# A two-layer trunk on one core: modulation split over three engines, norm rows between the first chains, last gate inside the first output tile, steps and loads moved

## The chip, the cores and the metric

The kernel runs on 1 core of one Trainium2 chip. TensorE (PE) multiplies, VectorE (DVE), ScalarE (ACT) and GpSimd (POOL) work on tiles in SBUF and PSUM, SyncE (SP) issues most DMAs. The metric is the device time of the core in microseconds (us), as the median of several executions.

## The reference

Two layers over 2080 tokens (a prompt of 2048 and a sample of 32) of width D = 1024. Every layer is `x + gate * rmsnorm(mixer(rmsnorm(x) * (1 + scale) + shift))`; shift, scale and gate come from the conditioning vector through one matrix `ada_w` of 1024 x 3072 a layer. Layer 0 mixes with a real-gated linear recurrence, layer 1 with forgetting attention.

```python
shift, scale, gate = split(silu(c) @ ada_w[i] + ada_b[i], 3)
h = rmsnorm(x, norm_pre[i]) * (1 + scale) + shift
# layer 0: 12 blocks of 128 of 1536 channels
xb, g = split(h @ lru_w_in, 2)
xc = conv4(xb)
r, ig = sigmoid(xc @ w_a + b_a), sigmoid(xc @ w_x + b_x)   # block by block
a = exp(-8 * r * softplus(-lam))
hs = scan(a, sqrt(1 - a * a) * ig * xc)
y = (hs * silu(g)) @ lru_w_out
# layer 1: 16 heads of 64, the sample also sees a cache of 512 rows
q, k, v, g, fl = split(h @ fox_w_in)
cum = cumsum(log_sigmoid(fl + b_f))
y = (softmax(q k^T / 8 + cum_q - cum_k, causal) @ v * silu(g)) @ fox_w_out
x = x + gate * rmsnorm(y, norm_post[i])
```

## The kernel before

**Precision.** A matrix is split into a rounded part (hi) and the rest (lo). `hi_pool` (L98, POOL) or `hi_act` (L95, ACT) writes hi, `lo_dve` (L104, a subtraction with two SBUF inputs on DVE) writes lo. A product is three matmuls: hi x hi, lo x hi, hi x lo, of 128 columns by 512.

**Order.** The code is written as generators which one Python program steps by hand; `yield` is a place where other work may be issued. A scheduler then places instructions by their dependences and by when buffers come free. Buffers come from pools with few slots each (roles `ahalf` 11 slots, `w` 5, `raw` 3, `half` 5, `h` 32, `c` 12, `wg` 2); a tile waits until the slot's last reader is done. Every engine and SP's queue run in order.

**0 to 56 us: first modulation.** `ada(0, (0, 2, 1, 3))` reads 32 tiles of 128x512 of `ada_w` (L243), with 8 loads ahead. Every third tile is `whole`: PE takes it as plain fp32 (L296 with `scf`). The other 21 are split: hi on POOL, lo on DVE, two matmuls each (L296 with `scs`). After 8 tiles `finish` adds (L259, L260), PE transposes the result (L269) and DVE writes the scales `gsv` (L276) or shifts `shv`. `prenorm` loads the first 1024 rows of `x` in four groups of 256, takes sums of squares (`stats`, L346 to L350), scales the rows (L353), transposes them on PE (L372), modulates them on ACT (L378) and splits them into `h`.

**56 to 729 us: layer 0's input.** `lru_in` runs over 12 blocks for each half of the tokens: `chain` (L556, 24 matmuls for 512 tokens), `gates` (L569), activations and the scan. Beside it run `norm_ahead` (norms the second half's rows into DRAM), `mod` (the rest of the modulations), `cache_parts` (splits the K and V cache), and `load_wout` (reads and splits w2, the output matrix of layer 0).

**729 to 1095 us: output of layer 0.** `out_tiles` takes 17 tiles of 128 tokens: 72 matmuls (L725) over 12 blocks into two banks (`pj`, `st`), as 36 pairs; `z` of a tile is loaded and split one tile ahead. When a tile is done, `norm_tile` norms its rows for layer 1: DVE writes `xn` (tile `c`, L445), PE transposes it in eight steps (L452) between the next tile's matmuls. The last modulation, layer 1's gate (`last`, 16 plain fp32 matmuls L296 into `pvb`), is stepped beside this.

**1095 to 2885 us: layer 1.** `proj` (V in L962, Q, K and gates in L1001) runs for the first half, then merged with attention. Attention is 640 steps of a 128-key tile each: scores (L1181, L1185), exponent on ACT (L1187, L1188), lo on DVE (L104), hi x hi sum on POOL (L1210), values (L1233, L1234). A unit's queries come by `q_load` into `ahalf` slots; its maxima (L1147) need `ext_d`, a DRAM tile. `LOAD_STEPS` is how many steps of the main stream pass between a job's loads and its first maxima. From 2680 us on, `out_tiles` of layer 1 (L725, tiles 0 to 6) run beside the last attention steps, with weights from `load_wout(w3)`; ten more tiles follow alone.

## Time and profile before

| | |
|---|---|
| median of 3 executions | 3035.75 us (3032.63 to 3041.42) |
| profiled execution, its own time | 3031.66 us |
| span of the profiled execution | 3029.7 us |
| PE busy in it | 2869.4 us, 95% |
| DVE, ACT, POOL busy | 1837.2, 1465.3, 1255.6 us |
| mean granted clock of PE | 0.985 |

The span is the time from the first to the last instruction of one execution. Where PE is busy 95% of it, time can be gained by closing what PE waits for, by fewer matmuls, or in stretches where its clock was granted below 1.00.

### The profile page before, as it was taken

What the parts mean: (1) busy time and instruction counts of PE and PEld (TensorE: products, weight loads), DVE (VectorE), ACT (ScalarE), POOL (GpSimd) and SP (SyncE); (2) the same over time, 40 slices, a digit from 0 to 9 for tenths busy, and PEclk for the clock granted to TensorE, in tenths of its full rate; (3) what the DMA queues carried; (4) which work ended last, traced back from release to release, by engine and by line L of the source; (5) the groups of instructions that cost most, each with busy time, mean ns of one, the idle gap of its engine ahead of it and who ended that gap; (6) DMA issues with size and microseconds to landing.
All of it is one profiled execution on the core that took longest, in us unless ns stands there. A gap on an engine that the chain in (4) does not pass through costs nothing.

```text
span 3029.7 us, 45098 instructions
## 1 busy us (share of the span) xinstructions
PE 2869.4 (95%) x14948; PEld 2293.8 (76%) x14948; DVE 1837.2 (61%) x3282; ACT 1465.3 (48%) x2962; POOL 1255.6 (41%) x1166
## 2 busy tenths in 40 slices
PE   6999999999999989999999999999999999989998
PEld 3777788897666677777777677887888788766776
DVE  7688777777432335646554565766776676676622
ACT  4565544556333333535354443665566556555621
POOL 5445443333222232434343332554555545455632
PEclk9999999999999999999999999999999999998999
DMA  7565675443644587676776776556555556464243
GB/s 277 197 220 199 218 270 192 151 152 127 191 135 129 161 302 254 187 247 187 222 220 210 227 222 192 147 176 154 152 155 152 165 148 176 131 164 121 82 135 96
DMA packets 407002, 548.40 MB, mean 181 GB/s; under 512 B 77096, under 2 KB 241064, under 8 KB 406768
## 3 DMA queue, kind: packets, MB, share of 16 engines
q1 hardware_dynamic: 406768, 545.50, 59.1%
q8 instruction: 119, 1.95, 0.3%
q14 instruction: 115, 0.94, 0.1%
HBM read 333.13 MB, written 212.22 MB: 180 GB/s over the span
## 4 chain that ended last, share of the span: by engine, by line
PE 38%; DMA 8%; DVE 6%; issue 5%; POOL 4%; ACT 3%; SPq 1%; POOLq 0%; DVEq 0%; ACTq 0%
PE pj L1001 13%; PE pj L962 4%; PE mx L1147 4%; PE st L1185 3%; PE st L1181 3%; PE pva L1233 3%; PE pvb L1234 3%; DVE ahalf L104 2%; DMA rc<-dn_d 1%; POOL ahalf L1210 1%; DVE mxs L1150 1%; PE pj L725 1%; DMA ahalf<-q_d 1%; POOL half L754 1%; PE mx L1376 1%
## 5 line engine op out<-in xcount | busy, mean ns | idle before, releaser
L1210 POOL TENSOR_TENSOR ahalf<-ahalf,ahalf 128x512 f32<-128x512 f32 (+2 forms) x528 | 582.5, 1103 | 418.7 <-ACT ahalf L1187 405.1
L1001 PE MATMUL pj<-h,w 128*128 128x512 f32 (+1 forms) x2304 | 585.3, 364 | 1.2 <-DVE half L104 1.2
L1187 ACT ACTIVATE ahalf<-st 128x512 fp32r<-128x512 f32 (+3 forms) x640 | 341.3, 533 | 376.0 <-PE st L1185 327.7
L104 DVE TENSOR_TENSOR ahalf<-st,ahalf 128x512 fp32r<-128x512 f32 (+3 forms) x640 | 386.9, 606 | 206.9 <-ACT st L1188 192.7
L1001 PEld LDWEIGHTS pj<-h,w 128*128 128x128 f32 x2304 | 424.5, 191 | 83.9 <-DVE half L104 1.4
L1150 DVE TENSOR_REDUCE mxs<-mx 128x1 f32<-128x512 f32 (+3 forms) x640 | 372.2, 605 | 148.0 <-PE mx L1147 84.9
L1188 ACT ACTIVATE st<-st 128x512 f32<-128x512 f32 (+3 forms) x640 | 339.8, 531 | 0.0
L1181 PE MATMUL st<-ahalf,kv 128*128 128x512 f32 (+3 forms) x640 | 244.0, 381 | 24.0 <-DVE ahalf L104 17.0
L1233 PE MATMUL pva<-ahalf,vs 128*128 128x512 f32 (+3 forms) x640 | 240.9, 388 | 10.8 <-POOL ahalf L1200 6.6
L962 PE MATMUL pj<-w,h 128*128 128x256 f32 (+3 forms) x1296 | 234.3, 288 | 12.1 <-DVE flog L977 5.4
L1185 PE MATMUL st<-ahalf,kb 96*128 96x512 f32 (+3 forms) x640 | 242.6, 386 | 1.0 <-ACT ahalf L1168 0.6
L1234 PE MATMUL pvb<-ahalf,vs 128*65 128x512 f32 (+3 forms) x640 | 228.1, 366 | 5.7 <-DVE od L1262 3.5
L1147 PE MATMUL mx<-kb,qm 96*128 96x512 f32 (+3 forms) x640 | 225.4, 384 | 7.2 <-DMA ext_d<-half 6.1
L556 PE MATMUL pj<-h,w 128*128 128x512 f32 (+1 forms) x1032 | 226.0, 369 | 0.8 <-POOL h L98 0.7
L962 PEld LDWEIGHTS pj<-w,h 128*128 128x128 f32 (+1 forms) x1296 | 192.3, 187 | 24.7 <-issue 7.5
L556 PEld LDWEIGHTS pj<-h,w 128*128 128x128 f32 x1032 | 177.3, 192 | 32.6 <-POOL h L98 0.9
L104 DVE TENSOR_TENSOR ahalf<-ahalf,ahalf 128x512 fp32r<-128x512 f32 (+2 forms) x183 | 143.9, 788 | 92.6 <-ACT ahalf L95 59.1
L104 DVE TENSOR_TENSOR w<-raw,w 128x1024 fp32r<-128x1024 f32 (+3 forms) x85 | 104.7, 1232 | 150.1 <-ACT w L95 68.5
L1001 PE MATMUL pj<-h,raw 128*128 128x272 f32 (+1 forms) x576 | 188.5, 327 | 0.0
L98 POOL TENSOR_SCALAR w<-raw 128x1024 fp32r<-128x1024 f32 (+3 forms) x68 | 76.1, 1120 | 251.5 <-DMA raw<-in_wqkg 54.2
L725 PE MATMUL pj<-h,ahalf 128*128 128x512 f32 (+1 forms) x408 | 168.2, 413 | 10.4 <-DVE ahalf L104 5.4
L1181 PEld LDWEIGHTS st<-ahalf,kv 128*128 128x128 f32 x640 | 121.7, 190 | 69.2 <-DVE ahalf L104 37.8
(325 smaller groups left out, 5615.5 us busy)
## 6 DMA issues: line engine op xcount, KB each, us to landing
wp_d<-w SPq DMA_DIRECT2D x60, 512.0 KB
vs<-v_d SPq DMA_DIRECT2D x96, 256.0 KB
kv<-k_d SPq DMA_DIRECT2D x192, 128.0 KB
ahalf<-q_d SPq DMA_DIRECT2D x192, 128.0 KB
raw<-in_w SPq DMA_DIRECT2D x44, 512.0 KB
ahalf<-in_ada_w SPq DMA_DIRECT2D x64, 256.0 KB
hb_d<-wg SPq DMA_DIRECT2D x32, 512.0 KB
v_d<-half SPq DMA_DIRECT2D x64, 256.0 KB
```

Of the source, the lines that this page charges most:

```text
L104: dve.tensor_tensor(o, i, f(h), ALU.subtract)
L556: pe.matmul(ps[:, :b - a], l, cols(r, a, b), start=i == 0, stop=i == 23)
L962: pe.matmul(ps[:m, :nw], l, r, start=c == 0, stop=c == 23)
L1001: pe.matmul(ps[:, :b - a], l, cols(r, a, b), start=c == 0, stop=c == 23)
L1147: pe.matmul(ps[:sw, :kw], u.qm[0:96, s0:s0 + sw], kb, start=True, stop=not last)
L1150: dve.tensor_reduce(u.mxs[:sw, si, c:c + 1], ps[:sw, :kw], axis=AX.X, op=ALU.max)
L1181: pe.matmul(ps[:kw, c0:nq], j.ka[k0 // 512][:, kc:kc + kw], u.qa[:, c0:nq], start=True, stop=False)
L1185: pe.matmul(ps[:kw, c0:nq], j.kb[k0 // HALF][0:96, kd:kd + kw], u.qb[0:96, c0:nq], start=False, stop=True)
L1187: act.activation(ph[:kw, c0:nq], ps[:kw, c0:nq], AF.Exp, scale=0.125)
L1188: act.activation(ps[:kw, c0:nq], ps[:kw, c0:nq], AF.Exp, scale=0.125)
L1210: pool.tensor_tensor(u.acc[:kw, c0:nq], f(ph)[:kw, c0:nq], u.acc[:kw, c0:nq], ALU.add)
L1233: pe.matmul(u.pva[:, c:nq], vs[:kw, 0:128], ph[:kw, c:nq], start=ti == 0, stop=last)
```

## The change

Nothing of the arithmetic's amount changes, but for the first modulation's `whole` tiles.
- First modulation: no tile is whole. All 32 get hi on ACT; lo is on POOL for tiles 0, 3, 6, ... (11 tiles, a two-input subtraction, new) and on DVE for the other 21.
- Rows of the first half: groups 2 and 3 are loaded before the first modulation ends into `c` slots, their stats follow group 1, and their transposes are issued between the matmuls of the first chains (`fill`).
- `norm_ahead` and `cache_parts` load one or two pieces ahead, the cache into `ahalf` slots (`cx`).
- `out_tiles`' first load and split stand ahead of the tail of layer 0's last block; the last gate's weights go into `w` slots, five ahead, and one of its matmuls is stepped per k (before, one per three).
- `norm_tile` has two more yields between `xn` and its transposes.
- The loads of `h` for V are spread: the first 512 tokens in the last output tile, the others between V steps.
- `LOAD_STEPS` 10 to 18, `q_load` two steps earlier, and w3 loaded two ahead with pauses, from the last projection unit on; two pauses ahead of the first output tile of layer 1.

```diff
...
-ADA_FIRST, ADA_LAST = 8, 6
+ADA_FIRST, ADA_LAST = 8, 5
...
-LOAD_STEPS = 10
+LOAD_STEPS = 18
...
                     a, b = get("ap", [128, 512], F32R), get("ap", [128, 512], F32R)
-                    hi_pool(a, t)
+                    (hi_act if ahead > 6 else hi_pool)(a, t)
+                    if ahead > 6 and i % 3 == 0:
+                        pool.tensor_tensor(b, t, f(a), ALU.subtract)
+                        parts[i] = (a, b)
+                        return
                     lo_dve(b, t, a)
...
                 for i in range(np_):
-                    x = get("xn", [w, pw])
+                    x = get("xn" if gi < 2 else "any", [w, pw])
                     sp.dma_start(x, src[t0 + 128 * t:t0 + 128 * t + w, pw * i:pw * i + pw])
...
-        ahead = 2
-        for gi in range(ahead):
+        for gi in range(2):
             load(gi)
-        done = 0
+        for gi in range(2):
+            stats(gi)
+        yield 0.0
+        for gi in range(2, len(groups)):
+            load(gi)
+        yield 0.0
         for gi, (t0, n, w) in enumerate(groups):
-            while done < min(gi + (1 if gi == 1 else 2), len(groups)):
-                stats(done)
-                done += 1
-            yield 0.0
+            if gi == 2:
+                stats(2)
+                stats(3)
+                yield 0.0
             xn = [xq.pop((gi, t)) for t in range(n)]
...
                 yield 110 * n
-            if gi + ahead < len(groups):
-                load(gi + ahead)
             flags.add(("n", layer, half, gi))
...
         groups = [(HALF + 256 * g, 2, 128) for g in range(4)] + [(SEQ, 1, NS)]
-        for t0, n, w in groups:
+        rows = []
+        def load(t0, n, w):
             xs = [[get("ahalf", [w, 512]) for _ in range(2)] for _ in range(n)]
...
                     sp.dma_start(xs[t][i], src[t0 + 128 * t:t0 + 128 * t + w, 512 * i:512 * i + 512])
-            yield
+            rows.append(xs)
+        load(*groups[0])
+        yield
+        for gi, (t0, n, w) in enumerate(groups):
+            xs = rows.pop(0)
             ss, rs = sm([128, 2, 2], "ss"), sm([128, 4], "rs")
...
                     dve.tensor_scalar(xs[t][i], xs[t][i], rs[:w, t:t + 1], None, ALU.mult)
+            if gi + 1 < len(groups):
+                load(*groups[gi + 1])
             g = 1 if t0 == SEQ else 0
...
         yield
+        yield
+        yield
         for k0 in (0, 4):
...
-    def lru_in(half, h, bank, gbank, lc, before):
+    def lru_in(half, h, bank, gbank, lc, before, fill=None):
...
                     i += 1
+                if fill is not None:
+                    next(fill, None)
...
         load(0)
+        yield 0.0
         if not half:
...
-    def load_wout(src, kn, w):
+    def load_wout(src, kn, w, ahead=0):
+        raw = {}
+        def load(k):
+            if k < kn:
+                raw[k] = get("raw", [128, D])
+                sp.dma_start(raw[k], src[128 * k:128 * k + 128, :])
+        for k in range(ahead):
+            load(k)
+        if ahead:
+            yield 0.0
         for k in range(kn):
-            t = get("raw", [128, D])
-            sp.dma_start(t, src[128 * k:128 * k + 128, :])
+            if not ahead:
+                load(k)
+            t = raw.pop(k)
             if k >= 8:
...
                     (hi_pool if k % 2 else hi_act)(a, t[:, c])
+                    if ahead:
+                        yield 1500.0
                     lo_dve(b, t[:, c], a)
...
                 w[i][k] = [p[i] for p in prs]
-            yield 0.0
+            del t, a, b, prs
+            if ahead:
+                load(k + ahead)
+            yield 1500.0 if ahead else 0.0
...
         load(0)
+        yield 2 * pause
+        yield 2 * pause
         split(0)
+        yield 0.0
         end = None
...
+        todo = [("k", p, 0) for p in range(NP)] + [("v", t, c) for t in range(PAST // 128) for c in range(4)]
+        raw = {}
+        def load(i):
+            if i < len(todo):
+                kind, t, c = todo[i]
+                if kind == "k":
+                    raw[i] = get("cx", [128, PAST])
...
+            del x
+            load(i + 2)
+            yield
...
             ws = wsp.pop(i)
-            done = False
+            if i == len(run_units) - 1:
+                flags.add(("last", half))
+                yield 0.0
...
             qm_load(u)
-            lds = [(max(0, late - 4), lambda: q_load(u))]
+            lds = [(max(0, late - 6), lambda: q_load(u))]
             m, tail = max_steps(u)
...
         set_roles(first, "wg", N_WG, "wg")
-        set_roles(first, "c", N_C, "any", "gp", "wout", "ap", "ab")
+        set_roles(first, "c", N_C, "any", "gp", "wout", "ap")
+        set_roles(big, "half", N_HALF, "ab")
         set_roles(big, "ahalf", N_AH, "z", "zs", "xn", "hf")
         set_roles(big, "h", N_H, "aw")
+        set_roles(big, "ahalf", N_AH, "cx")
         setup()
...
         next(pre)
-        run(ada(0, (0, 2, 1, 3), bank0, bank0, ADA_FIRST, lambda i: i % 3 == 0))
+        run(ada(0, (0, 2, 1, 3), bank0, bank0, ADA_FIRST))
         set_roles(big, "ahalf", N_AH, "aw", "ap")
-        set_roles(big, "half", N_HALF, "ab")
...
         wout = load_wout(io["w2"], NB, w)
-        blocks = lru_in(0, h, bank0, bank1, lc, rest)
+        def between():
+            for i in range(16):
+                for _ in range(0 if i < 6 else 1 + (i % 5 in (0, 1, 3))):
+                    next(pre, None)
+                yield
+        blocks = lru_in(0, h, bank0, bank1, lc, rest, between())
+        next(blocks)
+        next(pre)
+        next(blocks)
         run(until(pre, ("n", 0, 0, 1)))
-        next(blocks)
         next(blocks)
...
         run(parts)
+        set_roles(big, "w", N_W, "aw")
+        gps = {0: None, 1: None}
+        tiles = list(range(8)) + [16] + list(range(8, 16))
+        out = out_tiles(tiles, NB, z_d, io["x"], x1_d, gps, bank0, w, post=lambda t, o2: norm_tile(t, o2, bank1))
+        next(out)
         last = ada(1, (4, 5), bpvb, bank0, ADA_LAST, lambda i: True)
-        next(last)
         for _ in range(4):
             next(wout)
+        next(out)
+        next(out)
         for fn in rest:
...
         run(wout)
-        gps = {i: load_gp(0, i) for i in range(2)}
+        gps.update({i: load_gp(0, i) for i in range(2)})
         ones_rows()
         h = new_h()
-        tiles = list(range(8)) + [16] + list(range(8, 16))
-        out = out_tiles(tiles, NB, z_d, io["x"], x1_d, gps, bank0, w, post=lambda t, o2: norm_tile(t, o2, bank1))
         for i in range(16 * NB):
             next(out)
-            if i % 3 == 0:
-                next(last, None)
+            next(last, None)
         run(last)
...
             if k < KD:
-                for g in range(2):
-                    run(load_h(h, hb_d, g, 512 * g, 512, [k]))
+                run(load_h(h, hb_d, 0, 0, 512, [k]))
         tail = run(out)
+        loads = load_h(h, hb_d, 1, 512, 512)
         del w, gps, out
...
             next(tail, None)
+            next(loads, None)
+            next(loads, None)
         run(tail)
+        run(loads)
         pbank[0] = bpj
...
             yield next(b)
+        yield from until(b, ("last", 1))
+        w = [{}, {}]
+        wout = load_wout(io["w3"], NP, w, 2)
+        yield next(wout)
         yield from b
-        w = [{}, {}]
-        yield from load_wout(io["w3"], NP, w)
+        yield from wout
         gps = {0: load_gp(1, 0)}
...
```

How three places read in PE's order, before and after. First PE where the first chain starts; `pj` is the first chain's bank, `pva` and `mx` take transposes of normed rows (`ahalf`), `w` holds weights. In the kernel before:

```order
L372 MATMUL mx_613<-ident,ahalf_196 128x128
L372 MATMUL mx_613<-ident,ahalf_200 128x128
L372 MATMUL mx_620<-ident,ahalf_196 128x128
L372 MATMUL mx_620<-ident,ahalf_200 128x128
L556 MATMUL pj_700<-h_494,w_681 128x512
L556 MATMUL pj_700<-h_495,w_681 128x512
L556 MATMUL pj_700<-h_494,w_682 128x512
L556 MATMUL pj_700<-h_503,w_681 128x512
```

The changed kernel at the same place:

```order
L380 MATMUL mx_683<-ident,ahalf_194 128x128
L380 MATMUL mx_683<-ident,ahalf_198 128x128
L573 MATMUL pj_755<-h_593,w_574 128x512
L380 MATMUL mx_690<-ident,ahalf_196 128x128
L380 MATMUL mx_690<-ident,ahalf_200 128x128
L573 MATMUL pj_755<-h_594,w_574 128x512
L380 MATMUL pva_697<-ident,ahalf_196 128x128
L380 MATMUL pva_697<-ident,ahalf_200 128x128
L573 MATMUL pj_755<-h_593,w_575 128x512
```

Behind: the chain starts after the third of the four transposed pairs of group 1 and goes on between them; the transposes of groups 2 and 3, which stood behind the second chain, now stand between its matmuls.

Second, PE where the last chain of layer 0 meets the first output tile (`pj` and `st` there; weights `h`, `z` in `ahalf`; `pvb` is the last gate, `pva` and `mx` the last block's gates). In the kernel before:

```order
L296 MATMUL pvb_6118<-ahalf_6629,scs 34x512
L296 MATMUL pvb_6118<-ahalf_6630,scs 34x512
L725 MATMUL pj_7001<-h_6637,ahalf_6983 128x512
L725 MATMUL pj_7001<-h_6638,ahalf_6983 128x512
L296 MATMUL pvb_6845<-ahalf_6831,scf 34x512
L569 MATMUL pva_6889<-c_6791,half_6280 128x354
L569 MATMUL mx_6894<-c_6791,half_6280 128x354
L569 MATMUL mx_6899<-c_6791,half_6280 128x354
L296 MATMUL pvb_6845<-ahalf_6833,scf 34x512
```

The changed kernel at the same place:

```order
L573 MATMUL st_6823<-h_3472,wg_6357 128x272
L573 MATMUL st_6823<-h_3470,wg_6358 128x272
L765 MATMUL pj_7036<-h_6705,ahalf_6928 128x512
L765 MATMUL st_7037<-h_6707,ahalf_6928 128x512
L765 MATMUL pj_7036<-h_6706,ahalf_6928 128x512
L765 MATMUL st_7037<-h_6708,ahalf_6928 128x512
L765 MATMUL pj_7036<-h_6705,ahalf_6929 128x512
L765 MATMUL st_7037<-h_6707,ahalf_6929 128x512
L300 MATMUL pvb_7060<-w_7048,scf 34x512
```

Behind: before, two matmuls of output tile 0 stood ahead of the last block's gates and the rest behind them; now tile 0's first k stands whole ahead of a gate matmul of the last modulation and of the last block's gates, and further k between these.

Third, PE in the middle of an output tile, where the transposes of the tile before start (`mx` from tile `c`). The weights `h_6851` before are of k = 4, `h_6910` after of k = 6. In the kernel before:

```order
L725 MATMUL st_7281<-h_6852,ahalf_7205 128x512
L725 MATMUL pj_7280<-h_6849,ahalf_7206 128x512
L725 MATMUL st_7281<-h_6851,ahalf_7206 128x512
L452 MATMUL mx_7333<-ident,c_7306 128x128
L725 MATMUL pj_7280<-h_6859,ahalf_7205 128x512
L725 MATMUL st_7281<-h_6861,ahalf_7205 128x512
```

The changed kernel at the same place:

```order
L765 MATMUL st_7352<-h_6913,ahalf_7272 128x512
L765 MATMUL pj_7351<-h_6910,ahalf_7273 128x512
L765 MATMUL st_7352<-h_6912,ahalf_7273 128x512
L469 MATMUL mx_7426<-ident,c_7374 128x128
L765 MATMUL pj_7351<-h_6920,ahalf_7272 128x512
L765 MATMUL st_7352<-h_6922,ahalf_7272 128x512
```

Behind: the first transpose of a tile stands behind 21 pairs of matmuls, before behind 15; in the other steady tiles the same six pairs.

The numbers of matmuls on PE behind the last attention matmul differ too: 588 of L725 before, 738 after (L765); after, the output tiles of layer 1 start at attention step 578, 639 and 640 (before at 565, 587, 613 and 640).

## Rows read from the trace of the kernel before

**Rows 1.** the page: span, and the busy time of TensorE (PE)
```profile
span 3029.7 us, 45098 instructions
...
PE 2869.4 (95%) x14948; PEld 2293.8 (76%) x14948; DVE 1837.2 (61%) x3282; ACT 1465.3 (48%) x2962; POOL 1255.6 (41%) x1166
```

**Rows 2.** busy time by stretch: start:end length, each engine, PEclk, DMA share, GB/s
```profile
0.00:25.00 25.00, 11.07 (x24) 3.04 (x24) 14.90 (x58) 8.78 (x21) 8.97 (x21) 1.00 0.82 269
25.00:50.00 25.00, 19.64 (x71) 6.26 (x70) 23.11 (x34) 3.96 (x8) 19.09 (x21) 0.93 0.69 252
50.00:75.00 25.00, 22.08 (x90) 15.46 (x90) 17.10 (x39) 18.20 (x42) 13.91 (x26) 0.79 0.89 319
```

**Rows 3.** what PE waited for, 0 to 100 us: total, times, longest
```profile
PE st L269 <- DVE c L260: 3.1, 1, 3.1
```

**Rows 4.** PE in order of time, 40 to 100 us: start, length
```profile
45.87 0.42 PE L296 MATMUL pj<-c,scs 128*34 128x512 f32 x1 [1.40 <-DVE c L104]
...
56.50 7.54 PE L556 MATMUL pj<-h,w 128*128 128x512 f32 x24
...
88.06 5.71 PE L556 MATMUL pj<-h,w 128*128 128x512 f32 x24
```

**Rows 5.** the splits' tile c in 0 to 50 us, on POOL: ns min/median/max
```profile
L98 POOL TENSOR_SCALAR c<-h x21: 612/625/1128, 14.4 to 41.5; 128x512 fp32r<-128x512 f32 x21
```

**Rows 6.** the same tile on DVE
```profile
L104 DVE TENSOR_TENSOR c<-h,c x21: 672/1016/1518, 15.1 to 44.3; 128x512 fp32r<-128x512 f32 x21
```

**Rows 7.** POOL's two-input subtraction in attention, 2100 to 2500 us, by shape
```profile
L1210 POOL TENSOR_TENSOR ahalf<-ahalf,ahalf 128x512 f32<-128x512 f32 x114 | 146.8, 1287 | 91.3 <-ACT ahalf L1187 89.2
```

**Rows 8.** what PE waited for, 100 to 725 us
```profile
PE pva L569 <- ACT c L570: 8.1, 4, 2.5
```

**Rows 9.** busy time by stretch around the first output tile
```profile
725.00:750.00 25.00, 21.50 (x90) 12.63 (x90) 22.39 (x33) 15.84 (x22) 8.74 (x6) 0.86 0.43 138
750.00:775.00 25.00, 15.75 (x56) 10.97 (x55) 18.31 (x22) 11.77 (x14) 8.24 (x4) 0.80 0.57 184
```

**Rows 10.** what PE waited for, 725 to 775 us
```profile
PE pj L725 <- DVE ahalf L104: 5.4, 1, 5.4
PE pj L725 <- ACT ahalf L95: 5.0, 2, 3.8
PE pvb L296 <- DVE half L259: 2.3, 1, 2.3
```

**Rows 11.** what PE waited for, 775 to 1100 us (output tiles of layer 0)
```profile
PE mx L452 <- DVE c L445: 9.1, 8, 1.2
PE pva L452 <- DVE c L445: 6.3, 6, 1.3
```

**Rows 12.** a stretch of the last output tiles, all engines
```profile
2900.00:3000.00 100.00, 100.00 (x434) 81.23 (x433) 28.25 (x46) 20.88 (x49) 31.18 (x29) 1.00 0.47 143
```

**Rows 13.** what PE waited for, 1100 to 1130 us
```profile
PE pj L962 <- DVE flog L977: 5.4, 3, 4.8
```

**Rows 14.** what PE waited for, 1725 to 1860 us
```profile
PE mx L1147 <- DMA ext_d<-half: 6.1, 1, 6.1
```

**Rows 15.** what PE waited for, 1860 to 2600 us
```profile
PE st L1181 <- DMA ahalf<-q_d: 4.6, 5, 1.9
```

**Rows 16.** busy time by stretch, end of attention
```profile
2675.00:2900.00 225.00, 206.59 (x947) 156.27 (x948) 152.09 (x285) 123.53 (x260) 130.21 (x115) 0.95 0.42 117
2775.00:2800.00 25.00, 23.49 (x102) 17.91 (x103) 17.40 (x34) 15.03 (x35) 16.43 (x14) 0.80 0.42 124
```

**Rows 17.** what PE waited for, 2675 to 2900 us
```profile
PE st L1181 <- DVE ahalf L104: 5.3, 4, 3.2
PE pj L725 <- DVE half L753: 3.6, 3, 3.3
...
PE pj L725 <- ACT w L95: 1.8, 1, 1.8
```

More of the change, by code (lines that the diff above doesn't have):

```diff
@@ L766, in cache_parts @@
     def cache_parts():
-        for p in range(NP):
-            x, ab = get("raw", [128, PAST]), get("w", [128, 2, PAST], F32R)
-            a, b = ab[:, 0, :], ab[:, 1, :]
-            sp.dma_start(x, io["ckT"][p])
-            yield
-            hi_pool(a, x)
-            yield
-            lo_dve(b, x, a)
-            for n, y in enumerate((a, b)):
-                sp.dma_start(k_d[n, p, :, SEQ:SEQ + PAST], f(y))
-        for t in range(PAST // 128):
-            for c in range(4):
-                x, v2 = get("raw", [128, 4, 64]), get("w", [128, 4, 2, 64], F32R)
-                sp.dma_start(x, io["cv"][128 * t:128 * t + 128, 256 * c:256 * c + 256])
-                yield
+        todo = [("k", p, 0) for p in range(NP)] + [("v", t, c) for t in range(PAST // 128) for c in range(4)]
[5 more added lines that the diff above has]
+                    raw[i] = get("cx", [128, PAST])
+                    sp.dma_start(raw[i], io["ckT"][t])
+                else:
+                    raw[i] = get("cx", [128, 4, 64])
+                    sp.dma_start(raw[i], io["cv"][128 * t:128 * t + 128, 256 * c:256 * c + 256])
+        load(0)
+        load(1)
+        yield
+        for i, (kind, t, c) in enumerate(todo):
+            x = raw.pop(i)
+            if kind == "k":
+                ab = get("w", [128, 2, PAST], F32R)
+                a, b = ab[:, 0, :], ab[:, 1, :]
+                hi_pool(a, x)
+                yield
+                lo_dve(b, x, a)
+                for n, y in enumerate((a, b)):
+                    sp.dma_start(k_d[n, t, :, SEQ:SEQ + PAST], f(y))
+            else:
+                v2 = get("w", [128, 4, 2, 64], F32R)
                 hi_pool(v2[:, :, 1, :], x)
@@ L1627, in hybrid_kernel @@
         wout = load_wout(io["w2"], NB, w)
-        blocks = lru_in(0, h, bank0, bank1, lc, rest)
+        def between():
+            for i in range(16):
+                for _ in range(0 if i < 6 else 1 + (i % 5 in (0, 1, 3))):
+                    next(pre, None)
+                yield
+        blocks = lru_in(0, h, bank0, bank1, lc, rest, between())
+        next(blocks)
+        next(pre)
+        next(blocks)
         run(until(pre, ("n", 0, 0, 1)))
-        next(blocks)
         next(blocks)
```

## The prediction

> **What bounds the kernel now.** I read the profile's page first: PE is busy 2869.4 of a span of 3029.7 us [rows 1], so the span is the work of PE and 160 us in which it stands still, and the other engines count only where PE waits for them. Then I looked for those 160 us, with the stretches of busy time and with PE's waits in the same stretches. They lie in five places.
> - The start: PE is busy 11.07 and 19.64 us of the first two stretches of 25, then 22.08 at a granted clock of 0.79 [rows 2]. The first chain shows what the clock costs: 24 matmuls took 7.54 us, the same 24 later 5.71 [rows 4].
> - The first output tile of layer 0: 3.50 and 9.25 us idle in two stretches, clocks 0.86 and 0.80 [rows 9], and three waits that sum to 12.7 us, two of them for the split of `z` [rows 10].
> - Every output tile of layer 0: PE waits for `xn` ahead of its transposes, 9.1 and 6.3 us together, never longer than 1.3 [rows 11].
> - Two single waits between the projections and attention: 4.8 us for a slot at the end of V [rows 13], 6.1 us for `ext_d` at the second half's first maxima [rows 14].
> - The end of attention: 206.59 of 225 us busy, and the clock 0.95 over it, 0.80 in one stretch of it [rows 16].
>
> Where PE never waits, a matmul of 512 columns costs 0.23 us: 434 in 100 us [rows 12]. That is my price of PE work below.
>
> **The sum** is made against the profiled execution, 3031.66 us by its own clock for a span of 3029.7; the median of the runs shown is 3035.75, 4.1 above it, and I add these 4.1 at the end.
>
> **First modulation and first chains: -5 us.** PE's part: 11 whole fp32 tiles become 22 split matmuls, shorter in sum, and none is on the path, since PE waits for splits there: the last of them stood 1.40 us for DVE's lo [rows 4]. Removed are 21 hi on POOL; added are 32 hi on ACT, which was busy 3.96 of 25 us there [rows 2], and 11 lo on POOL. DVE's 21 lo stay. DVE was busy 23.11 of 25 us [rows 2], so it set the pace, but its subtraction took 0.672 us at best and 1.016 in the median [rows 6]: something held it up, and POOL's copies, 0.612 at best and up to 1.128 [rows 5], were held up too. Their excess over the best, 21 x (1.016 - 0.672), is 7 us.
> If moving hi to ACT frees DVE, some 5 of these 7 come back; the chain after it gains too, since it starts behind three of the four pairs of transposes of group 1 and no longer behind all, and the transposes of groups 2 and 3 fill the second chain: of the 2.9 us idle and 0.21 x 25 = 5.3 us of clock lost in the third stretch [rows 2] I count 5. That makes -10.
> If two-input subtractions on POOL and DVE exclude each other, POOL's 11 take 1.287 us each, the duration of POOL's subtraction beside a busy DVE in attention [rows 7]: 14.2 us plus 21 x 0.672 = 14.1, together 28.3, against 21 x 0.625 + 14.1 = 27.2 before [rows 5, 6]. The modulation then ends where it did or 1 us later, and only 3 to 4 of the chain's 5 stay: -3. The median of 1.016 lies nearer to this case than to freedom, so I take -5. The lower bound is -14 (all idle and clock of the third stretch as well), the upper +4 (below, as a rival).
> The Trainium skill has a rule for it ("SBUF — State Buffer", Who interferes with whom): DVE and GpSimd share one pair of ports under an exclusive lock, and a DVE instruction with two SBUF inputs contends with a GpSimd instruction that reads SBUF. By that rule moving hi off POOL helps little while a longer two-input operation takes its place, and the term would be -3; the stretched durations of both engines agree with it, but no row shows two subtractions of this shape side by side.
> The tail is unchanged: two splits of `w` and `wg` still stand on DVE before the last `gsv`, behind a 3.1 us wait of PE [rows 3].
>
> **Layer 0's input: -2 us.** `norm_ahead` and `cache_parts` issue the same operations, their loads earlier. PE's waits for the gates' `c` sum to 8.1 us in 100 to 725 us [rows 8]; a part of these stood behind such operations on DVE. I take a quarter, with -8 and +2 as bounds: the cache pieces now sit in `ahalf` slots, which the gates want too.
>
> **First output tile: -12 us.** In PE's order tile 0 now starts right behind the chains and its matmuls fill the holes between the last block's gates, and the splits of `z` stand a block earlier on ACT and DVE. If that holds, the 12.7 us of waits [rows 10] shrink to under 1. The clock could give more, 0.14 x 25 + 0.20 x 25 = 8.5 us at most [rows 9], so -17 with half of it. The other bound is -4: ACT's share of the waits, 5.0, goes, and the gate's chain stays.
>
> **Transposes later in the tile: -15 us.** The same transposes of the steady tiles are issued, six pairs later: 12 x 0.23 = 2.8 us, more than the longest wait, 1.3 [rows 11]. Nothing is added but that `xn` holds its `c` slot 2.8 us longer. So all 15.4 us go but a remnant; bounds -16 and -8 (half stays, if the slots of `c` or `wg` come free too late for DVE).
>
> **V's start: 0 us.** The loads of `h` are spread, but the long wait there is for a `half` slot [rows 13], which no edit touches. Bounds -5 (it goes, DMA being less crowded) and +5 (it doubles).
>
> **Half switch: -5 us.** Eight more main steps of three matmuls, 8 x 3 x 0.23 = 5.5 us, stand before the maxima that waited 6.1 us [rows 14]. Bounds 0 and -6.
>
> **Queries two steps earlier: 0 us.** To gain are 4.6 us [rows 15]; to lose, two `ahalf` slots of eleven held longer in each unit, while attention's own waits are for those slots' writers. Bounds -5 and +6.
>
> **End of attention: 0 us.** w3's splits are spread, so the 1.8 us wait for ACT's `w` and part of the other waits [rows 17] should go. But 738 matmuls of output tiles stand behind the last attention matmul where 588 stood: 150 x 0.23 = 34.5 us of PE work leave the phase. If attention then runs that much faster, nothing is lost: the phase of 225 us must end in 190. DVE, busy 152 us [rows 16], POOL, 130, and ACT, 124, would allow it; DVE would be at 80%. I take that, with -12 (half of the idle and the clock come back) and +20 (attention gives back 15 of 34.5) as bounds.
>
> Together: -5 - 2 - 12 - 15 + 0 - 5 + 0 + 0 = -39; 3031.66 - 39 + 4.1 = 2997 us.
>
> **The rivals.**
> - *POOL's subtractions lock DVE out.* Before, hi and lo overlapped in part, else DVE could not have been busy 23.11 us beside 19.09 of POOL in 25 [rows 2]. If 11 x 1.287 = 14.2 us of POOL exclude DVE fully, where some 5 of the 7 us of holding up reached the end before, the modulation ends 14.2 - 5 = 9 us later, and the start costs 9 - 5 = +4 with the chain's gain, in place of -5: 3006 us. For it: the stretched medians [rows 5, 6]. Against it: ACT's hi lets POOL run far ahead of DVE's need.
> - *The first output tile still waits.* The last gate's weights go into `w` slots, whose loads stand on SP's queue ahead of the last pieces of w2; a load that waits for PE there holds w2 up. Then -3 in place of -12: 3006 us. Against it: w2's last pieces are wanted only at k = 11, 66 matmuls or 15 us into the tile.
> - *The yields do not reach.* If `xn` waits for DVE behind work that moves with it, 4 of 15.4 us are gained: 3008 us. Against it: only PE's instructions moved in the order, and no wait is above 1.3 us.
> - *Attention alone keeps its pace* (the slower side). If each of its last steps is held by the chain from score over ACT, DVE and POOL to value, taking work away from PE saves no time, and the 34.5 us come on top; PE, with more holes, falls to a clock such as 0.80 [rows 16] in place of 0.95 over some 90 us of the phase, 14 us more. 2997 + 48 = 3045. For it: 61 of the last 62 steps have one output tile beside them. Against it: half of PE's waits there are for the fill's own operands [rows 17]. It decides the sign where the phase loses the 39 us gained elsewhere, that is, if it does not get shorter than 229 us.
>
> **How the numbers follow.** Forecast 0.53, lock 0.20, first tile 0.12, yields 0.07, attention's pace 0.08. The forecast's own bounds, added as independent, give 2981 to 3013. The range takes in the three rivals up to 3008 with the same spread on them, and leaves out attention's pace and the last of the gains: 2974 to 3021. A difference under 0.3% (9.1 us) can hardly be told from none. Of the forecast and the first three rivals (0.92), 0.89 stay more than that below 3035.75 and 0.03 end within it, where two of them meet; attention's pace gives 0.03 within and 0.05 above. So faster 0.89, same 0.06, slower 0.05.
>
> **What the profile after would show.** Start: the first chain before 52 us (56.50 before), and `c<-h,c` on DVE back at 0.67 us in the free case, at 1 us under a lock. First tile: no wait for L95 or L104 above 1 us in 725 to 775 us. Tiles: the wait of the transposes for `xn` under 2 us in all. Half switch: no wait for `ext_d`. End: PE idle no more than 20 us from the last projection to the last attention step, and the clock not below 0.93. Wrong would be the sum if PE's idle time in that phase passes 40 us, or if new waits of the scores for query loads or `ahalf` slots exceed 10 us.

## The result, and the profile after

The changed kernel takes 3014.64 us (median of 4 executions, 3012.26 to 3017.04) against 3034.19 us for the kernel before on the same chip: a ratio of 0.9932, 95% interval 0.9912 to 0.9952. That is 19.5 us saved where 39 were forecast; the time lies inside the range given, 2974 to 3021, and on its slow side.

The page of the profiled execution (its own time 3012.26 us), in the form of [rows 1]:

```profile
span 3010.5 us, 45166 instructions
...
PE 2860.8 (95%) x14948; PEld 2290.1 (76%) x14948; DVE 1843.2 (61%) x3282; ACT 1488.2 (49%) x2996; POOL 1257.2 (42%) x1156
```

PE still stands idle for 150 us. Where the 19 us lie is read from PE's order of time: I took the end of the n-th matmul of a line as a mark (the start, for the first of a line) in both traces, and subtracted.

| stretch, in us | before | changed | difference | forecast |
|---|---|---|---|---|
| start to the end of the fourth chain | 88.2 | 88.8 | +0.6 | -5 |
| to the end of the first half's chains | 294.6 | 301.8 | +7.2 | -2 with the next |
| to the end of the second half's chains | 346.7 | 351.2 | +4.5 | |
| to the end of output tile 1's matmuls | 67.8 | 59.4 | -8.4 | -12 |
| to the end of the last output tile of layer 0 | 298.6 | 273.0 | -25.6 | -15 |
| to the first projection | 33.9 | 36.7 | +2.8 | 0 |
| to the last projection | 1569.6 | 1561.8 | -7.8 | -5 |
| to the end | 330.3 | 337.8 | +7.5 | 0 |

Both output terms came, one larger than forecast. The losses are in the stretches that I had put down as small gains or as nothing. The last two rows belong together: from the first projection to the end the kernel before takes 1899.8 us and the changed kernel 1899.7, so what one row gains the other loses. Between these two executions the whole saving lies ahead of the first projection.

**The start.** Busy time by stretch, for [rows 2], then PE in order of time, for [rows 4]:

```profile
0.00:25.00 25.00, 9.65 (x27) 3.58 (x27) 18.34 (x60) 16.34 (x33) 8.31 (x16) 1.00 0.82 276
25.00:50.00 25.00, 17.07 (x63) 6.37 (x62) 20.27 (x27) 13.61 (x27) 16.77 (x14) 0.85 0.80 293
50.00:75.00 25.00, 19.86 (x93) 14.96 (x94) 20.28 (x42) 17.67 (x42) 14.37 (x27) 0.74 0.62 219
```

```profile
50.17 0.64 PE L300 MATMUL pj<-c,scs 128*34 128x512 f32 x1 [1.23 <-DVE c L104]
54.48 0.59 PE L273 MATMUL st<-ident,half 2*128 2x2 f32 x4 [3.67 <-DVE half L264]
...
58.76 0.80 PE L573 MATMUL pj<-h,w 128*128 128x512 f32 x1 [0.29 <-POOL h L98]
```

The modulation's last matmul starts at 50.17 us (45.87 before) and the first chain at 58.76 (56.50 before). The clock granted in the third stretch is 0.74, where it was 0.79, and PE is busy 19.86 us of it, where it was 22.08. The tile `c` of the splits, on DVE and on POOL (minimum, median, maximum), for [rows 5, 6]:

```profile
L104 DVE TENSOR_TENSOR c<-h,c x21: 671/679/1775, 17.8 to 48.6; 128x512 fp32r<-128x512 f32 x21
```

```profile
L254 POOL TENSOR_TENSOR c<-h,c x11: 1270/1284/2849, 14.1 to 45.1; 128x512 fp32r<-128x512 f32 x11
```

DVE's median is back at 0.68 us, but single ones take 1.78, and POOL's subtraction, 1.28, takes up to 2.85. The prediction had named DVE's duration as the sign that tells its two cases apart (0.67 us free, 1 under a lock). The median says free; the longest durations and the late start say otherwise.

**Output of layer 0.** Stretches around the first tile, for [rows 9], then what PE waited for from 775 to 1075 us, for [rows 11]:

```profile
725.00:750.00 25.00, 24.91 (x150) 20.22 (x148) 24.35 (x33) 15.49 (x25) 10.89 (x9) 1.00 0.56 176
750.00:775.00 25.00, 22.90 (x86) 14.05 (x86) 23.74 (x24) 16.76 (x19) 13.89 (x6) 1.00 0.62 198
```

```profile
PE pj L765 <- POOL c L98: 1.8, 1, 1.8
```

The transposes' 15.4 us of waits are gone, the clock at the first tile is full, and of 12.75 us of idle there 2.2 are left.

**Layer 1.** PE's longest wait around V's start, 1065 to 1130 us, for [rows 13]:

```profile
PE pj L1020 <- DVE flog L1035: 6.5, 2, 5.3
```

What PE waited for from 1690 to 1860 us, for [rows 14], and from 1860 to 2600, for [rows 15], there one more line of the kernel before and then the changed one:

```profile
PE st L1243 <- ACT ahalf L1226: 3.7, 3, 2.7
PE mx L1205 <- DMA qm<-q_d: 3.3, 1, 3.3
```

```profile
PE st L1181 <- DVE ahalf L104: 7.4, 5, 2.5
```

```profile
PE st L1239 <- DVE ahalf L104: 10.3, 8, 2.2
```

No wait for `ext_d` is left there, but the maxima wait 3.3 us for another load, `qm`. The waits for query loads (4.6 us) are gone, and the scores' wait for DVE's `ahalf` rose from 7.4 to 10.3.

The end of attention, a stretch as long as the one in [rows 16], one slice of it, and PE's waits there, for [rows 17]:

```profile
2625.00:2850.00 225.00, 196.65 (x914) 144.82 (x913) 157.61 (x296) 130.43 (x275) 131.78 (x117) 0.94 0.44 111
2700.00:2725.00 25.00, 18.32 (x71) 12.51 (x69) 16.18 (x29) 12.16 (x22) 14.75 (x14) 0.86 0.57 113
```

```profile
PE st L1239 <- DVE ahalf L104: 10.1, 12, 5.8
PE pva L1291 <- ACT ahalf L1245: 7.3, 5, 5.2
PE pvb L1296 <- ACT ahalf L95: 5.4, 3, 3.7
```

PE is busy 196.65 us where it was 206.59. From the last projection (2673 us) to the first output tile (2714 us) the attention steps stand alone for 41.5 us, and PE waits for their own chain: scores for DVE, values for ACT. Before, it was 10.0 us (2699 to 2709; the first output tile of layer 1 does not start at 2680, as I wrote ahead). The signs that the prediction gave for this phase held all the same: from the last projection to the last attention matmul PE idles 17.2 us of 153.5 (12.4 of 182.0 before), where 20 was the limit named, and the clock is 0.96 (0.94 before).

### The profile page after: what moved, and what is told of

It reads as the page before. It is cut to its first block, busy times and chain, and to the rows that moved or that the text cites. A ratio compares the mean times of both kernels' runs of the same rounds, so it can differ in the third digit from the quotient of the medians.

```text
span 3010.5 us, 45166 instructions
## 1 busy us (share of the span) xinstructions
PE 2860.8 (95%) x14948; PEld 2290.1 (76%) x14948; DVE 1843.2 (61%) x3282; ACT 1488.2 (49%) x2996; POOL 1257.2 (42%) x1156
## 5 line engine op out<-in xcount | busy, mean ns | idle before, releaser
L573 PE MATMUL st<-h,wg 128*128 128x512 f32 (+1 forms) x840 | 187.6, 377 | 2.3 <-DVE wg L104 1.5
L104 DVE TENSOR_TENSOR w<-raw,w 128x1024 fp32r<-128x1024 f32 (+2 forms) x61 | 86.6, 1420 | 153.5 <-ACT w L95 92.0
L573 PEld LDWEIGHTS st<-h,wg 128*128 128x128 f32 x840 | 147.8, 192 | 32.1 <-DVE wg L104 2.7
```

Of the source, the lines that this page charges most:

```text
L104: dve.tensor_tensor(o, i, f(h), ALU.subtract)
L573: pe.matmul(ps[:, :b - a], l, cols(r, a, b), start=i == 0, stop=i == 23)
```

## The experiments

Each ran beside the kernel before on one chip; ratios are to that. The kernel before took 3039.07 us beside e1 to e4, 3037.28 beside e5 to e8 and 3031.93 beside e9 to e12, so medians of different groups, and the changed kernel's 3014.64, are compared by their ratios. Differences between medians of one group are of the size of their spread where they are under about 4 us, so stretches of the traces are read beside them.

**The start: what made it later?** Three edits to `split` and `finish` of the first modulation, and one that adds work.

```diff
# e1_start_old
-                    (hi_act if ahead > 6 else hi_pool)(a, t)
-                    if ahead > 6 and i % 3 == 0:
...
+                    hi_pool(a, t)
...
+        run(ada(0, (0, 2, 1, 3), bank0, bank0, ADA_FIRST, lambda i: i % 3 == 0))
```

> The changed kernel, but with the first modulation split as before (hi on POOL, lo on DVE, every third tile whole as fp32); the order of rows and chains stays as changed. Theory (ACT's in-order queue: the hi of the next column stands behind the copy of the finished sum, which waits for PE, and POOL's lo stands behind that): the modulation ends at 46 us again and not at 50, the first chain starts at about 54 instead of 58.8, and the time is 4 to 6 us below the changed kernel's 3014.6, about 3009. Rival (the start is late because of the interleaved rows, or the ports that DVE and POOL share are the limit either way): the first chain starts at 58 or later, and the time stays within 2 us of 3014.6.

3009.83 us, ratio 0.9906 (0.9886 to 0.9926). The first chain starts at 56.2 us, against 58.8 to 61.0 in seven traces with the changed start; the fourth chain ends at 86.7 us, 1.5 before the kernel before. So the new split lost 2.6 to 4.8 us at the first chain, and what else changed at the start won 1.5 by the fourth chain's end. The time is near the 3009 us of a theory that the next two runs refute. The start fits neither theory nor rival: the modulation's last matmul starts at 47.9 us, where I expected 46, and that stands 2 us behind the kernel before with the same split as there; what causes these 2 us was not tested.

```diff
# e5_copy_dve
-            act.activation(lo, ps[32:34, :], AF.Copy)
+            (hi_dve if ahead > 6 else hi_act)(lo, ps[32:34, :])
```

> The changed kernel, but in the first modulation the copy of a finished column's lower rows out of PSUM runs on DVE and not on ACT. Theory (the copies of hi on ACT stand in order behind that copy, which waits for PE): the gaps of ACT before the copy (1.9, 2.7 and 0.7 us before the first three) vanish from its hi, the modulation ends at 46 to 47 instead of 50 us, the first chain starts 3 us earlier. Rival (the ports that DVE and POOL share, or POOL's 1.28 us of lo behind each third hi): the modulation ends at 49 to 51 us as in the changed kernel.

3019.19 us, ratio 0.9949 (0.9931 to 0.9967). The first chain starts at 60.3 us. Nothing was gained. The copy now stands in DVE's order in place of ACT's, so this run alone does not clear ACT; the next one does, since it leaves ACT's hi and the copy in ACT's order and still starts early. With it my theory of ACT's queue fell.

```diff
# e6_lo_dve
                     (hi_act if ahead > 6 else hi_pool)(a, t)
-                    if ahead > 6 and i % 3 == 0:
-                        pool.tensor_tensor(b, t, f(a), ALU.subtract)
-                        parts[i] = (a, b)
-                        return
```

> The changed kernel, but all 32 lo of the first modulation are on DVE, none on POOL (hi stays on ACT). Theory of shared ports: without two-input subtractions on POOL, DVE's lo keep 0.67 us throughout, 32 x 0.67 = 21.4 us fit between 14 and 46 us, and the modulation ends at 46 to 47. Rival (ACT's order): no earlier than 49, since hi still waits behind ACT's copy of the sums; DVE, with 11 x 0.67 = 7.4 us more to do, may make it 51.

3008.06 us, ratio 0.9916 (0.9893 to 0.9940). The modulation's last matmul starts at 48.2 us, the first chain at 55.3: the shortest start so far, with the most work on DVE. Its lo, 32 of them:

```profile
L104 DVE TENSOR_TENSOR c<-h,c x32: 669/686/1445, 16.0 to 47.4; 128x512 fp32r<-128x512 f32 x32
```

```diff
# e12_dummy_pool: as e6_lo_dve, and
+                    if ahead > 6 and i % 3 == 0:
+                        if "s" not in spare:
+                            spare["s"] = get("ahalf", [128, 512], F32R)
+                        pool.tensor_tensor(spare["s"], t, f(a), ALU.subtract)
```

> The kernel with all 32 lo of the first modulation on DVE, and beside them POOL makes the same 11 subtractions into a spare tile that nothing reads (extra work, for nobody). Theory (two-input subtractions on POOL and DVE shut each other out): DVE's lo are stretched again, maximum 1.7 us and more, and the first chain starts 2 us or more behind the 55.3 us of the run without them. Rival (in the changed kernel it was PE's and the path's wait for POOL's slow lo, not the ports): the first chain starts within 1 us of 55.3.

3017.64 us, ratio 0.9950 (0.9934 to 0.9967); the first chain starts at 64.6 us, 9.2 behind e6_lo_dve. DVE and POOL in order of time, in this run:

```profile
37.83 6.41 DVE L104 TENSOR_TENSOR c<-h,c 128x512 fp32r<-128x512 f32 x5
```

The first and the second of these five, and the last:

```profile
37.83 1.62 DVE L104 TENSOR_TENSOR c<-h,c 128x512 fp32r<-128x512 f32 x1
39.38 1.78 DVE L104 TENSOR_TENSOR c<-h,c 128x512 fp32r<-128x512 f32 x1
42.48 1.76 DVE L104 TENSOR_TENSOR c<-h,c 128x512 fp32r<-128x512 f32 x1
```

```profile
35.90 3.01 POOL L256 TENSOR_TENSOR ahalf<-h,c 128x512 fp32r<-128x512 f32 x1 [4.65 <-ACT c L95]
39.08 1.52 POOL L256 TENSOR_TENSOR ahalf<-h,c 128x512 fp32r<-128x512 f32 x1 [0.18 <-POOL ahalf L256]
...
42.01 1.68 POOL L256 TENSOR_TENSOR ahalf<-h,c 128x512 fp32r<-128x512 f32 x1 [0.59 <-POOL h L98]
```

Five lo that take 0.67 us each alone, 3.4 in sum, took 6.41 while POOL ran subtractions whose result nobody reads, and POOL's own took up to 3.01 here, and 5.63 earlier, in place of 1.27. The order of their ends says that one waits for the other: each of the three long lo ends 0.55 us behind the end of one of POOL's three subtractions (38.91, 40.60 and 43.69 us). The two engines shut each other out; that is shown by durations, not by waits. Not all of the 9.2 us need be that: POOL's useful hi of `w` and `h` stand in order behind the useless ones, and the hi tile's slot is kept until POOL has read it.

**The layer-0 input: who lost 12 us?**

```diff
# e2_norm_old: norm_ahead and cache_parts are those of the kernel before
# e7_norm_ahead_old: norm_ahead alone
-        load(*groups[0])
-        yield
...
-            if gi + 1 < len(groups):
-                load(*groups[gi + 1])
# e8_next_later
         next(later)
+        next(later)
```

> The changed kernel, but with norm_ahead and cache_parts as before (loads at the old places, cache pieces in the three raw slots). Theory (these two cost the layer 0 input its 10 us: earlier loads hold ahalf slots and put DVE's row scaling behind other work): the last chain ends about 9 us earlier than the changed kernel's 741.8, the time is about 3006. Rival (the loss comes from the last modulation's steps, which now fall a block earlier, or from the start): the last chain ends within 3 us of 741.8 and the time within 3 us of 3014.6.

> The changed kernel, but norm_ahead alone as before (each group's loads right ahead of its use); cache_parts stays as changed. Theory (norm_ahead's earlier loads cost the first half, the cache's earlier loads help the second): the 1st half of layer 0's input takes 294.5 us from the end of the fourth chain to the end of the half's last, as before (295) and not 302, the second half stays at 351, and the time is 6 us below 3014.6. Rival (it is the cache's new place in ahalf slots that costs the first half): the first half stays at 302, time within 2 us of 3014.6.

> The changed kernel, but the second half's block generator is stepped once more ahead of the loop that steps it together with the modulations and the cache pieces, so that these run one step behind where the change put them. Theory (the modulations, now a step earlier against the blocks, wait for DVE, 3.3 and 3.8 us at layer 1's columns, and lower the clock): the second half of layer 0's input takes 347 us as before instead of 351, the time is 3 to 4 us below 3014.6. Rival (the waits there come from the cache's loads or chance): within 2 us of 3014.6.

3009.15 us (0.9907, 0.9884 to 0.9931), 3010.30 (0.9912, 0.9894 to 0.9930) and 3016.70 (0.9935, 0.9915 to 0.9955).

| stretch, in us | before | changed | e2 | e7 | e8 |
|---|---|---|---|---|---|
| first half (from the fourth chain) | 294.6 | 301.8 | 294.5 | 294.9 | 302.6 |
| second half | 346.7 | 351.2 | 358.1 | 351.1 | 349.4 |

With the old `norm_ahead` the first half's 7.2 us are back, in both (e2's trace is that of its longest execution, 3018.84 us). In e9 and e10 below, which have all lo on DVE besides, only 4 are: the half takes 298.3 and 298.6 us, against 302.5 in e6. In all four the half ends at 383.4 to 384.7 us, whether the first chain starts at 54.5 or at 61.0; what holds it there stays open. With the old `cache_parts` the second half loses another 7 (358.1 us in one trace; those with the earlier loads show 349.4 to 353.7), so the cache's earlier loads do help in this kernel. PE's idle time in the first half is 7.8 us in the changed kernel and 4.3 in e7, 3.5 of the 7.2 us. What PE waited for from 100 to 400 us, in the changed kernel and then in e7_norm_ahead_old, shows it:

```profile
PE mx L432 <- DVE ahalf L420: 1.7, 1, 1.7
...
PE pva L432 <- ACT ahalf L434: 1.0, 1, 1.0
PE st L573 <- POOL wg L98: 0.8, 1, 0.8
...
PE mx L432 <- ACT ahalf L434: 0.6, 1, 0.6
```

```profile
PE pva L579 <- ACT c L580: 1.9, 1, 1.9
PE st L564 <- DVE wg L104: 1.3, 1, 1.3
PE mx L579 <- ACT c L580: 0.8, 1, 0.8
```

The transposes of `norm_ahead` (L432) wait in the changed kernel, 3.3 us, and not in the other. The other half of the 7.2 us is in PE's busy time. e8's second half is 1.8 us shorter than the changed kernel's and the time does not follow: the second half's 4.5 us stay mostly open. The gain of e7 is 7.3 us at the last chain (734.5 for 741.8) and 2.1 in its profile's span: it lost 8.3 from the first projection to the last, a stretch for which the traces with the same code there show 1557 to 1570 us.

**The yields.**

```diff
# e3_no_yields
         yield
-        yield
-        yield
         for k0 in (0, 4):
```

> The changed kernel without the two added yields between the scaled rows and their transposes. Theory (the yields alone close the waits of the transposes): waits of the transposes for xn are back at 15 us in sum, and the time is 15 to 19 us above 3014.6, about 3031. Rival (the out tiles ran faster because the kernel starts them in another state, with z split earlier): less than 6 us above.

3038.21 us, ratio 1.0003 (0.9987 to 1.0020): without the two yields nothing of the change's gain is left. PE's waits in its output tiles, 780 to 1100 us:

```profile
PE mx L467 <- DVE c L460: 12.9, 10, 2.6
PE pva L467 <- DVE c L460: 6.0, 6, 1.2
```

They sum to 18.9 us. The stretch from tile 1 to the last output tile takes 294.3 us and 273.0 with the yields, 21.3 less: PE's idle time in just that stretch is 18.2 us and none with the yields, and the other 3 are in PE's busy time.

**Attention and its end.**

```diff
# e4_end_old
-        yield from until(b, ("last", 1))
-        w = [{}, {}]
-        wout = load_wout(io["w3"], NP, w, 2)
-        yield next(wout)
         yield from b
-        yield from wout
+        w = [{}, {}]
+        yield from load_wout(io["w3"], NP, w)
...
-        yield 2 * pause
-        yield 2 * pause
+        yield 0.0
+        yield 0.0
# e11_load_steps
-LOAD_STEPS = 18
+LOAD_STEPS = 10
```

> The changed kernel, but with w3 loaded and split as before (behind the last projection, without pauses) and no pause ahead of layer 1's first output tile. Theory (moving 150 output matmuls behind the last attention step leaves PE without filling: idle and a lower clock between 2625 and 2850 us): the time from the last projection matmul to the end is some 8 us shorter, the time about 3007. Rival (the loss there comes from the maxima and query steps, not from w3): the time stays within 3 us of 3014.6 or rises.

> The changed kernel with LOAD_STEPS 10. Theory (the eight steps remove the 6.1 us wait for ext_d and nothing else): a single wait of 5 to 6 us for ext_d is back between 1700 and 1860 us, the time is 5 us above 3014.6. Rival (the eight steps also push attention behind the projections and so lengthen the end, 337.8 us from the last projection to the end against 330.3 before): the end is 3 to 7 us shorter, and the time stays within 3 us of 3014.6.

3013.84 us (0.9918, 0.9901 to 0.9935) and 3011.11 (0.9929, 0.9912 to 0.9946): neither is told from the changed kernel by its time. From the last projection to the end, e4_end_old takes 335.7 us and e11_load_steps 331.8; the ten traces with the changed form of both take 335.1 to 340.5, the changed kernel 337.8. e4's form is thus not told from the changed one there either. In e11_load_steps no wait for `ext_d` returns. PE's longest waits there from 1690 to 1860 us:

```profile
PE pj L1020 <- DMA h<-hb_d: 6.8, 5, 3.7
PE mx L1205 <- DMA qm<-q_d: 3.1, 1, 3.1
```

So the wait that I wanted to remove had gone by something else, which was not found. What the eight steps do change is PE's idle time at the end: from the last projection to the last attention matmul it is 11.6 us in e11_load_steps, 12.4 in the kernel before, and 16.7 to 18.1 in the twelve traces with the eight steps. The stretch with no output tile is not what costs it: in e4_end_old that is 13.5 us long in place of 41.5, and PE idles 17.4 us. But these five us do not show in the time. From the first projection to the end e11_load_steps takes 1898.3 us and e4_end_old 1898.8; the changed kernel takes 1899.7, the kernel before 1899.8, and all traces of the experiments 1894.9 to 1906.1. No part of the change behind the first projection, nor all of it together, is told from nothing there.

**Together.** e9_lo_dve_norm is e6_lo_dve with the old `norm_ahead`; e10_plus_end takes the old end (e4_end_old) besides.

> The changed kernel with the two undoings that paid, together: all 32 lo of the first modulation on DVE, and norm_ahead as before. If the two losses lie in separate stretches and nothing later takes them back, the last chain of layer 0 ends at 730 to 732 us (before 729.5, changed 741.8), and the time is 3014.6 - 6.6 - 4.3 = about 3003.5. Rival (attention starts by other phases of the DMA queue and gives the gain back, as in the run with norm_ahead alone, where 9 us were lost between 1100 and 1850): the last chain ends early, but the time is 3008 to 3010.

> The kernel of the run before, and w3 loaded and split as before besides, with no pauses ahead of layer 1's output. If the last part of the change costs 3 us in the stretch from the last projection to the end (339 us as changed, 335.7 with the old form), the time is 3 us below that run's. If it is indifferent, within 2 us of it.

e9: 3007.06 us (2999.73 to 3008.04), ratio 0.9911 (0.9894 to 0.9928). The two undoings do not add, and the expectation missed: the last chain ends at 735.3 us and not at 730 to 732, where the old `norm_ahead` alone gives 734.5. The first chain starts at 55.2 us, 4.4 earlier than with that alone, and nothing of it is left at the last chain. e10: 2998.99 us (2996.94 to 3003.06), ratio 0.9891 (0.9873 to 0.9909), by ratio some 12 us below the changed kernel: the lowest of all, with an interval just clear of the changed kernel's (0.9912 to 0.9952). From the last projection to the end e10 takes 332.3 us, e9 336.0, but from the first projection e10 takes 1897.0 and e9 1894.9, so the old end is not shown to gain anything. The 8 us between their medians lie in the spread of e9, whose profiled execution has a span of 2998.0 us, below e10's:

```profile
span 2999.2 us, 45157 instructions
...
PE 2852.2 (95%) x14948; PEld 2289.0 (76%) x14948; DVE 1850.4 (62%) x3293; ACT 1486.1 (50%) x2994; POOL 1239.1 (41%) x1145
```

## Why the prediction was half right

- **What bounds it** was right: PE, and its waits. Of the 19.2 us between the two profiled executions 10.6 are less idle time of PE (160.3 before, 149.7 after) and 8.6 less busy time.
- **First modulation, -5: wrong in sign**, and it is the rival on POOL's subtractions that came, in part. The step that failed is the choice between the two ends: I took a value near the lock's, but reckoned that under the lock the modulation would end where it did or 1 us later. It ended 4.3 us later (50.17 for 45.87). The split alone cost 2.6 to 4.8 us (e1_start_old) and the interleaved rows with the rest of the start gave 1.5, not 4 to 5. The sentence "ACT's hi lets POOL run far ahead of DVE's need" was wrong: POOL's and DVE's subtractions met, and both grew. The rule of the Trainium skill that I weighed there ("SBUF — State Buffer", Who interferes with whom: a DVE instruction with two SBUF inputs contends with a GpSimd instruction that reads SBUF, under an exclusive lock) agrees with e12_dummy_pool: 6.41 us for five lo, the long ones ending behind POOL's.
- **Layer 0's input, -2: wrong, +11.7**, outside my bound of +2, and the largest error of the sum. I held that `norm_ahead` issued the same operations earlier. Its loads ahead cost the first half 7 us in two runs and 4 in two more, in which all lo are on DVE. I had named the slots as a danger for the cache's pieces, not for these; that it is the slots (each group holds four of eleven `ahalf`) is argued, not shown.
- **First output tile, -12: right in mechanism, near in number partly by luck.** PE's idle time between the last chain and the tile's end fell from 12.8 us to 0.8. The table's -8.4 has 14 gate matmuls more in it, which ran behind tile 1 before. The kernel without the yields is 4.3 us faster than the one before in the later tiles, so -8.4 - 4.3 = -12.7 for all but the yields. In that number the clock came back too (0.82 before from the last chain to the tile's end, 1.00 after), which the forecast had only as a bound, and the later tiles without the yields hold 3.0 us more idle time than before (18.2 for 15.2), which takes some of it away again. The rival of waiting `w` slots did not come.
- **Transposes later, -15: right in mechanism, mis-sized**: 21.3 by e3_no_yields. I summed the waits. Without the yields PE's idle time there was longer in the new kernel than before (18.2 us for 15.2), and closing it gave 3 us more than its sum, in PE's busy time.
- **V, 0**: +2.8 here, inside the bounds. The wait for a `half` slot stayed: 4.8 us before, 5.3 now.
- **Half switch -5, queries 0, end of attention 0: no gain came.** The rows show -7.8 and +7.5, but their sum from the first projection to the end is -0.2, where -5 was forecast. The waits for `ext_d` and for the queries went and nothing was gained by it; LOAD_STEPS does not carry the first, what does stays open. That -7.8 lies near -5 is luck: traces with the same code there show 1557 to 1570 us, and the kernel before, 1569.6, lies within. For the end I held that attention gives back the 34.5 us that were moved behind it. PE's time behind the last attention matmul grew by 36.1 us (148.2 to 184.3), and the phase ahead of it shrank by 28.5 (182.0 to 153.5): the rival of attention's own pace came to a fifth, inside the bound of +20, and does not show in the time from the first projection on. A reading in that rival holds for the rows shown alone: of all PE's waits from 2675 to 2900 us, 19 us, 5.4 are for operands of the output tiles, under a third and not half.
- **The range.** The bounds of the eight terms, added as independent, give 18 us down and, without the 20 of attention's rival, 17 up, where 16 stand on both sides of 2997. The measured time lies just above that, and inside the range by the part that was added for the rivals.

The sum of the misses: +5.6 at the start, +13.7 in layer 0's input, +3.6 and -10.6 in the output tiles, +2.8 at V, -2.8 and +7.5 behind the first projection, together +19.8: the 39 forecast less the 19.2 between the two profiled executions.

## What to carry to other kernels

Before work is moved to an idle engine, ask what both engines read: two-input subtractions on POOL and DVE held each other up here, and leaving all 32 on one busy engine started the first chain earlier than sharing them. Follow such a gain to the next place where PE waits: with the old `norm_ahead` it was gone by the last chain. Read neighbouring stretches together before one of them is called a gain. Loading further ahead is not free, for whatever reason it was so here; test each such edit alone, since two of them here went opposite ways. A short wait that recurs in each tile adds up: moving the waiting instructions six pairs back in program order gave 21.3 us, as much as the whole change, and no wait appeared in its place.

## What was not expected of the hardware

- A useless stream of 11 subtractions of 1.27 us on POOL, read by nobody, went with a first chain at 64.6 us in place of 55.3; the slots that it holds may be part of that.
- Closing 18.2 us of PE's idle time ahead of transposes shortened the stretch by 21.3 us.
- Executions of one program differ by more than the terms argued over here: e2_norm_old took 3005.57 to 3018.84 us.
